# The entry of a feed-forward stage: four weight operands split ahead of the norm, three behind it, and the first products of two blocks put together

## The chip, the cores and the metric

The kernel runs on one core of a Trainium2 chip. The metric is the device time of one execution in microseconds (us); lower is better. The engines of the core work in parallel, each through its own queue in order: TensorE (PE, matmuls and transposes), VectorE (DVE), ScalarE (ACT), GpSimd (POOL) and SyncE (SP), which here only issues DMA transfers. Tiles live in SBUF (128 partitions), matmul results in PSUM (eight banks).

## The reference

One decoder layer on 512 tokens of width 1024, in float32: a time-mixing group and a sparse-attention group share one norm and one input projection, then comes the output projection and then a dense SwiGLU stage, in which the change lies:

```python
h = h + jnp.concatenate([y_r, y_n], axis=-1) @ w_out[l]
h = h + swiglu(rms_norm(h, norm_ffn[l]), w_gate[l], w_up[l], w_down[l])
return rms_norm(h, norm_final)

def rms_norm(x, g):
    y = xf * lax.rsqrt(jnp.mean(xf * xf, axis=-1, keepdims=True) + NORM_EPS)
    return (y * g.astype(jnp.float32)).astype(x.dtype)

def swiglu(x, w_gate, w_up, w_down):
    return (jax.nn.silu(x @ w_gate) * (x @ w_up)) @ w_down
```

The hidden width D_FF is 2816.

## The kernel before

**Split products.** Every float32 operand of a large product is split into a high half (rounded to a shorter float, by ScalarE, line 144) and a low half (the rest, by VectorE, line 146). `mm3` (lines 162 to 165) issues three matmuls for each pair: high by high, high by low, low by high. So each operand costs one ScalarE pass and one VectorE pass before TensorE can use it.

**The seven products.** The two matrices x @ w_gate and x @ w_up are formed together for 256 hidden columns at a time. The code calls such a piece a value of `q`; here it is called a block. There are eleven. For each, a Strassen-like scheme forms seven products in place of eight, of operands that are quarters or sums of quarters. On the activation side these are A11, A12, S1, S2, S3, S4 and A22, made once by `ffn_norm`. On the weight side they are B11, B21, T1, T2, T3, B22 and T4, made for each block by `weight_side`. The products of a block are taken in the order B11, B21, T2, T1, T3, B22, T4 (lines 1182 to 1203). `prod` issues 24 matmuls for each, into a PSUM bank of the tags pj, ra and s in turn. VectorE adds each result into the tiles u, g0, v and u1; ScalarE applies Silu.

**The norm.** `ffn_norm` is a generator; each step handles one tile of 128 tokens. ScalarE sums the squares (line 176) and takes the root (line 177), VectorE takes the reciprocal and then multiplies the rows by it and by the gain, which lies broadcast to all partitions in `gain2` (line 1072). TensorE transposes eight blocks of 128 (line 1082) into two ps_s banks, and ScalarE drains each bank in one pass of 512 columns into `raw` (line 1084). A11 and A12 are split from token tiles 0 and 1 directly. With tiles 2 and 3 the sums are formed by VectorE in place in `raw` (lines 1095 to 1100) and split one by one.

**The output projection ahead of it.** `accumulate` uses all eight PSUM banks: two for each token tile. For its last four blocks of rows it goes token tile by token tile and yields the tile's two banks. The caller adds them to `x2` (line 1159) and runs one step of the norm. `ahead` is called before that last part and traces `weight_side(0, 2)`: the loads of block 0, and its splits, of which the first two (B11, B21) get tiles of the tag b8 of their own. The other five use the tags whi and wlo, two buffers each, which the last weights of the output projection hold until its end.

**The loads of a block.** B11 and B21 are plain loads of w_gate into one tile of the tag wraw (three buffers), B22 a plain load of w_up into another. T1 and T3 are each a plain load from SyncE's queue and then, from GpSimd's queue, a load that adds in place (`accum_op`, lines 1137 and 1138). T2 = T1 + B22 and T4 = T2 + B21 are added by VectorE. For even blocks the tiles t1, t2, t3 have the tag t4 (four buffers), for odd blocks they are one large tile of the tag L (four buffers). The other L tiles at that time are `x2`, `raw`, `Aa` and the ring of the output projection, whose buffer `Ab` takes over.

**What orders the work.** Instructions are traced in program order. A planner that works with its own times for each instruction then puts them into the engines' queues, the earliest ready first and by priority; `tc.high_priority()` raises what is traced inside it. Before, the weight splits and the drains of the products have high priority, the norm does not. A tile of a tag waits until the last reader of the buffer's former tile is done.

## Time and profile before

| | |
|---|---|
| median of three runs | 770.64 us (769.45 to 771.62) |
| profiled execution | 770.73 us, span 769.0 us |
| TensorE busy | 738.6 us, 96% of the span, 6093 matmuls and transposes |
| VectorE, ScalarE, GpSimd busy | 543.3, 381.5 and 160.0 us |
| mean granted TensorE clock | 0.984 |
| moved by DMA | 82.83 MB, mean 108 GB/s |

The span runs from the first to the last instruction of the profiled execution; the time holds a little more around it. Starts of instructions are counted from the start of the span. A row of the timeline gives start, length, engine, line, operation, output and inputs with their shapes, how many such instructions it merges, and in brackets the engine's idle time before it and what ended that. A row of the waits gives who waited for whom, us in total, how often, and the longest. The chain of waits follows the work that ended last back from the end. In it, and in the groups, "L" is the name of a tile tag where it stands without a number, and a line of the code where a number follows. In the table of stretches the clock is that which the throttle granted to TensorE, 1.00 being full speed.

### The profile page before, as it was taken

Reading aid. Unit: us, or ns where it says so; the run is one execution under the profiler, and the core shown is the slowest. Engines: PE = TensorE matmul, PEld = TensorE weight load, DVE = VectorE, ACT = ScalarE, POOL = GpSimd, SP = SyncE. Lnnn points to the kernel's source line nnn. Section 1 sums busy time; section 2 is a strip of 40 time slices with the busy share of each in tenths; the row PEclk is TensorE's granted clock in tenths of the full one; section 3 lists DMA queues with packets and bytes.
Section 4 is the critical chain, followed back from the end, with each engine's and each line's share of the span. In section 5 each row is a group of like instructions: output and inputs, shape, how many; then the busy total and the mean of one; then the engine's idle time right before and its main releaser. Section 6 shows DMA issues by size and latency. Waiting matters only on the chain.

```text
span 769.0 us, 14989 instructions
## 1 busy us (share of the span) xinstructions
PE 738.6 (96%) x6093; PEld 648.1 (84%) x6093; DVE 543.3 (71%) x1052; ACT 381.5 (50%) x652; POOL 160.0 (21%) x258
## 2 busy tenths in 40 slices
PE   8999999998889999999996899999999999999996
PEld 7867888898877878867786899999999998888885
DVE  5488689789768987875659497888695994333235
ACT  7398643224277776676447344444443552233224
POOL 3210054058345542442001102020202000000000
PEclk9999999999989999999998999999999999999998
DMA  7722543100051000321218569696768444322102
GB/s 247 223 82 84 164 110 110 55 2 2 3 219 30 3 1 3 85 83 56 83 55 192 110 176 203 161 223 151 161 159 221 112 153 147 110 68 97 55 1 110
DMA packets 69243, 82.83 MB, mean 108 GB/s; under 512 B 4868, under 2 KB 62806, under 8 KB 69174
## 3 DMA queue, kind: packets, MB, share of 16 engines
q1 hardware_dynamic: 57558, 70.34, 28.5%
q0 software_dynamic: 11616, 11.54, 9.9%
q8 instruction: 48, 0.79, 0.4%
q14 instruction: 21, 0.17, 0.1%
HBM read 79.77 MB, written 2.10 MB: 106 GB/s over the span
## 4 chain that ended last, share of the span: by engine, by line
PE 74%; DVE 15%; DMA 6%; issue 2%; ACT 1%; POOL 0%; SPq 0%; DVEq 0%; POOLq 0%; ACTq 0%
PE ps_ra L165 7%; PE ps_ra L164 7%; PE ps_ra L163 6%; PE ps_pj L165 6%; PE ps_pj L163 6%; PE ps_pj L164 6%; PE ps_s L165 4%; PE ps_s L163 4%; PE ps_s L164 4%; PE ps_o L1001 3%; DVE wlo L146 3%; PE ps_pj L993 2%; DMA L<-in_w_up_dram 2%; DMA wraw<-in_w_up_dram 2%; DMA L<-in_w_gate_dram 2%
## 5 line engine op out<-in xcount | busy, mean ns | idle before, releaser
L144 ACT ACTIVATE whi<-wraw 128x1024 fp32r<-128x1024 f32 (+1 forms) x79 | 78.5, 1033 | 33.2 <-PE ps_s L165 8.2
L146 DVE TENSOR_TENSOR wlo<-wraw,whi 128x1024 fp32r<-128x1024 f32 (+1 forms) x62 | 77.7, 1284 | 14.9 <-ACT whi L144 11.3
L146 DVE TENSOR_TENSOR L<-b,L 128x512 fp32r<-128x512 f32 x24 | 16.2, 691 | 57.1 <-PE ps_rb L164 55.1
L990 POOL TENSOR_SCALAR whi<-whi,m,gates 128x128 f32<-128x128 f32 (+3 forms) x64 | 42.5, 679 | 36.9 <-DVE m L988 28.7
L144 ACT ACTIVATE L<-b 128x512 fp32r<-128x512 f32 x24 | 14.9, 632 | 70.0 <-PE ps_rb L164 65.1
L164 PE MATMUL ps_ra<-wlo,L 128*128 128x256 f32 (+1 forms) x140 | 47.6, 340 | 0.2 <-DVE wlo L146 0.2
L163 PE MATMUL ps_ra<-whi,L 128*128 128x256 f32 (+1 forms) x140 | 47.4, 340 | 0.2 <-ACT L L144 0.2
L165 PE MATMUL ps_ra<-whi,L 128*128 128x256 f32 (+1 forms) x140 | 47.0, 337 | 0.0
L165 PE MATMUL ps_pj<-whi,L 128*128 128x256 f32 (+1 forms) x140 | 46.3, 332 | 0.0
L164 PE MATMUL ps_pj<-wlo,L 128*128 128x256 f32 (+1 forms) x140 | 46.3, 331 | 0.0
L163 PE MATMUL ps_pj<-whi,L 128*128 128x256 f32 (+1 forms) x140 | 45.9, 332 | 0.0
L164 PE MATMUL ps_ra<-L,whi 128*128 128x256 f32 (+2 forms) x128 | 44.3, 346 | 1.0 <-DVE L L146 1.0
L163 PE MATMUL ps_ra<-L,whi 128*128 128x256 f32 (+2 forms) x128 | 44.1, 345 | 0.9 <-ACT L L144 0.9
L165 PE MATMUL ps_ra<-L,wlo 128*128 128x512 f32 (+2 forms) x120 | 41.2, 343 | 0.0
L987 ACT ACTIVATE whi<-whi,m 128x128 f32<-128x128 f32 (+3 forms) x64 | 35.4, 554 | 9.3 <-DVE m L986 8.1
L165 PE MATMUL ps_pj<-L,wlo 128*128 128x512 f32 (+1 forms) x112 | 38.8, 346 | 0.1
L163 PE MATMUL ps_pj<-L,whi 128*128 128x512 f32 (+1 forms) x104 | 36.3, 349 | 0.2 <-ACT whi L144 0.2
L164 PE MATMUL ps_pj<-L,whi 128*128 128x512 f32 (+1 forms) x104 | 35.9, 346 | 0.0
L986 DVE CUSTOM_DVE_ANT_0 whi<-ps_s,negb 128x128 f32<-128x128 f32 (+3 forms) x64 | 29.3, 484 | 5.9 <-PE ps_pj L993 2.5
L1137 POOL DMA_DIRECT2D t<-in_w_up_dram x6 | 7.9, 1322 | 115.1 <-DVE whi L146 50.4
L163 PEld LDWEIGHTS ps_ra<-whi,L 128*128 128x128 f32 x140 | 27.6, 197 | 3.1 <-ACT L L144 0.6
L164 PEld LDWEIGHTS ps_ra<-wlo,L 128*128 128x128 f32 x140 | 27.5, 196 | 3.0 <-DVE wlo L146 0.5
(627 smaller groups left out, 2462.4 us busy)
## 6 DMA issues: line engine op xcount, KB each, us to landing
wraw<-in_w_gate_dram SPq DMA_DIRECT2D x22, 512.0 KB
wraw<-in_w_down_dram SPq DMA_DIRECT2D x11, 1024.0 KB
wraw<-in_w_in_dram SPq DMA_DIRECT2D x9, 1024.0 KB
t<-in_w_up_dram POOLq DMA_DIRECT2D x12, 512.0 KB, 7.4
wraw<-in_w_up_dram SPq DMA_DIRECT2D x11, 512.0 KB
L<-in_w_up_dram POOLq DMA_DIRECT2D x10, 512.0 KB, 8.9
wraw<-in_w_out_dram SPq DMA_DIRECT2D x4, 1024.0 KB
wraw<-in_w_in_dram SPq DMA_DIRECT2D x6, 512.0 KB
```

Source lines behind the costliest of these rows:

```text
L144: ACT.activation(hi, src, AF.Copy)
L146: (POOL if pool else DVE).tensor_sub(lo, src, hi.bitcast(F32))
L163: PE.matmul(o, lh, rh, start=start, stop=False)
L164: PE.matmul(o, lh, rl, start=False, stop=False)
L165: PE.matmul(o, ll, rh, start=False, stop=stop)
L986: DVE.tensor_tensor_reduce(pr[:, i], pS[:, i], negb[:, S - n:S], scale=-1.0, scalar=3e38, op0=OP.add, op1=OP.min, accum_out=m[:, i, 0:1])
L987: ACT.activation(pr[:, i], pr[:, i], AF.Exp, scale=-1.0, bias=m[:, i, 0:1], accum_out=m[:, i, 1:2])
L990: POOL.tensor_scalar(pr[:, i], pr[:, i], m[:, i, 2:3], gv[:, 1 + b0 + i, h:h + 1], op0=OP.mult, op1=OP.mult)
L993: PE.transpose(pT[:, j], prr[:, x, j * 128:j * 128 + 128], ident)
L1001: PE.matmul(po[q, 2 * g:2 * g + 2], vtok[:, j % (t + 1), b0 + j // (t + 1), g], pTs[:, par, j], start=False, stop=g == 1 and bs[-1] == 1 a ...
L1137: POOL.dma_start(t1, quarter(w_up, 0), accum_op=OP.add)
```

## The change

- `t2` gets four buffers in place of three, and the scratch for DMA descriptors (`dynamic_dma_scratch_size`) is 2048 in place of 4096.
- The norm's weight `norm_ffn` is loaded as eight more of the small rows that are transposed at the start, so that it lies as one value for each partition; the broadcast tile `gain2` and its load go.
- In `ffn_norm` ScalarE multiplies the rows by the reciprocal root (a Copy with a scale), in place of VectorE. After the transposes ScalarE drains each block of 128 columns by a pass of its own, with the norm's weight as the scale: eight passes for each token tile in place of two.
- S1 gets a tile of its own and S3 is formed in place; the order of the splits is S2, S1, S3, S4, A22.
- `weight_side` becomes the class `Weights` with four parts: the constructor (loads of B11 and B21), `begin` (their splits), `load_rest` (the other loads), `middle` (T2 and T1), `end` (T3, B22, T4).
- For block 0, `ahead` splits B11, B21, T2 and T1, all into b8 tiles. `end` is traced after the norm, and its instructions on ScalarE and VectorE are queued behind the norm's last split.
- The additions to `x2` and the steps of the norm get high priority.
- The constructor and `begin` of block 1 are traced before that `end`, its other loads after block 0.
- The products go B11 and B21 of block 0, B11 and B21 of block 1, then the other five of block 0, the other five of block 1, and from block 2 on as before.

```diff
-    SB_BUFS = {"L": 4, "b8": 6, "t4": 4, "t2": 3, "wraw": 3, "whi": 2, "wlo": 2}
+    SB_BUFS = {"L": 4, "b8": 6, "t4": 4, "t2": 4, "wraw": 3, "whi": 2, "wlo": 2}
...
+                       ("norm_ffn", norm_ffn, 8)):
...
-    gain2 = st([128, D], "t4")
-    nc.sync.dma_start(gain2, bcast_row(norm_ffn))
...
+    last = []
     def ffn_norm(src):
...
-            DVE.scalar_tensor_tensor(xn, s, r, gain2, op0=OP.mult, op1=OP.mult)
+            ACT.activation(xn, s, AF.Copy, scale=r)
...
             def put(name, v):
-                split(v, A[name][0][:, :, c], A[name][1][:, :, c])
+                hi, lo = (o[:, :, c] for o in A[name])
+                last[:] = ACT.activation(hi, v, AF.Copy), DVE.tensor_sub(lo, v, hi.bitcast(F32))
...
-                ACT.activation(rv, p.rearrange("p (k n) -> p k n", n=128), AF.Copy)
+                for i in range(HK):
+                    ACT.activation(rv[:, i], p[:, i * 128:(i + 1) * 128], AF.Copy, scale=col("norm_ffn", kh * HK + i))
...
-                s3 = st([128, HK, 128], "t2")
-                DVE.tensor_sub(s3, a11, a21)
-                DVE.tensor_sub(a21, a22, a21)
-                DVE.scalar_tensor_tensor(a11, a21, -1.0, a11, op0=OP.mult, op1=OP.subtract)
+                s1 = st([128, HK, 128], "t2")
+                DVE.tensor_sub(s1, a22, a21)
+                DVE.tensor_sub(a21, a11, a21)
+                DVE.scalar_tensor_tensor(a11, s1, -1.0, a11, op0=OP.mult, op1=OP.subtract)
                 put("S2", a11)
-                put("S1", a21)
+                put("S1", s1)
+                put("S3", a21)
...
     def ahead():
-        first.append(weight_side(0, 2))
+        ws[0] = Weights(0)
+        ws[0].begin("b8")
+        ws[0].load_rest()
+        ws[0].middle("b8")
...
-        for f in range(2):
-            sl = slice(f * 512, f * 512 + 512)
-            DVE.tensor_add(x2[:, t, sl], banks[f], x2[:, t, sl])
-        next(norm)
+        with tc.high_priority():
+            for f in range(2):
+                sl = slice(f * 512, f * 512 + 512)
+                DVE.tensor_add(x2[:, t, sl], banks[f], x2[:, t, sl])
+            next(norm)
...
+    ws[1] = Weights(1)
+    ws[1].begin()
+    with tc.issue_after(last[0].ins), tc.issue_after(last[1].ins):
+        ws[0].end()
+    first_products(0)
+    first_products(1)
+    last_products(0)
+    for q in range(1, NF // 2):
+        if q > 1:
+            ws[q] = Weights(q)
+            ws[q].begin()
+        ws[q].load_rest()
+        ws[q].middle()
+        ws[q].end()
+        if q > 1:
+            first_products(q)
+        last_products(q)
```

`first_products(q)` holds the products with B11 and B21 and what follows them, `last_products(q)` the other five; their bodies are the lines 1181 to 1207 of before.

More of the change, by code (lines that the diff above doesn't have):

```diff
@@ L1150, in hybrid_layer, with __init__, quarter, put @@
-    first = []
+    class Weights:
+        def __init__(self, q):
+            def quarter(w, kh):
+                return w[kh * 512:kh * 512 + 512, q * 256:q * 256 + 256].rearrange("(k p) n -> p k n", p=128)
+            r = st([128, 2, HK, 256], "wraw")
+            self.b11, self.b21 = r[:, 0], r[:, 1]
+            nc.sync.dma_start(self.b11, quarter(w_gate, 0))
+            nc.sync.dma_start(self.b21, quarter(w_gate, 1))
+            self.q, self.quarter = q, quarter
+        def put(self, name, v, tag=None):
+            if tag is None:
+                tag = ("whi", "wlo")[turn2[0] % 2]
+                turn2[0] += 1
+            o = operand(tag)
+            split(v, *o)
+            setattr(self, name, o)
+        def begin(self, tag=None):
+            with tc.high_priority():
+                self.put("B11", self.b11, tag)
+                self.put("B21", self.b21, tag)
+        def load_rest(self):
+            self.b22 = st([128, 2048], "wraw")[:, 0:1024].rearrange("p (k n) -> p k n", n=256)
+            if self.q % 2:
+                tt = st([128, 4, HK, 256], "L")
+                self.t1, self.t2, self.t3 = (tt[:, i] for i in range(3))
+            else:
+                self.t1, self.t2, self.t3 = (st([128, HK, 256], "t4") for _ in range(3))
+            nc.sync.dma_start(self.t1, self.quarter(w_gate, 0))
+            nc.sync.dma_start(self.b22, self.quarter(w_up, 1))
+            nc.sync.dma_start(self.t3, self.quarter(w_up, 0))
+            with tc.high_priority():
+                POOL.dma_start(self.t1, self.quarter(w_up, 0), accum_op=OP.add)
+                POOL.dma_start(self.t3, self.quarter(w_up, 1), accum_op=OP.add)
+        def middle(self, tag=None):
+            with tc.high_priority():
+                DVE.tensor_add(self.t2, self.t1, self.b22)
+                self.put("T2", self.t2, tag)
+                self.put("T1", self.t1, tag)
+        def end(self):
+            with tc.high_priority():
+                self.put("T3", self.t3)
+                self.put("B22", self.b22)
+                DVE.tensor_add(self.t2, self.t2, self.b21)
+                self.put("T4", self.t2)
@@ L1198, in hybrid_layer @@
             DVE.tensor_add(u1, p, v)
-        p = prod(w["B22"], A["S4"])
+        p = prod(w.B22, A["S4"])
         with tc.high_priority():
@@ L1202, in hybrid_layer @@
         DVE.scalar_tensor_tensor(hq[:, :, 0:256], v, -1.0, g0, op0=OP.mult, op1=OP.mult)
-        p = prod(w["T4"], A["A22"])
+        p = prod(w.T4, A["A22"])
         with tc.high_priority():
```

72 lines of the change are left out of this document (21 added, 51 removed).

## The prediction

> **What bounds the kernel now.** The page comes first. Its row of TensorE (PE), busy tenths in 40 slices of 19.2 us:
>
> ```profile
> PE   8999999998889999999996899999999999999996
> ```
>
> Only a few stretches can give time back. The entry of the FFN, from 400 to 440 us, is too short to stand out in it. The table of stretches comes next (columns: stretch and its length, then busy us and instruction count of PE, PEld, DVE, ACT and POOL, then the granted clock, DMA share and GB/s):
>
> ```profile
> 405.00:410.00 5.00, 1.77 (x10) 1.21 (x10) 5.00 (x6) 5.00 (x10) 0.97 (x1) 0.98 0.60 158
> 410.00:415.00 5.00, 4.55 (x21) 4.55 (x22) 5.00 (x9) 2.14 (x6) 0.58 (x2) 0.50 1.02 269
> 420.00:425.00 5.00, 3.11 (x16) 2.71 (x17) 4.90 (x9) 4.28 (x7) 0.00 (x0) 0.85 0.33 53
> 435.00:440.00 5.00, 2.48 (x21) 2.27 (x20) 3.92 (x4) 1.06 (x1) 0.00 (x0) 1.00 0.74 119
> 460.00:480.00 20.00, 20.00 (x170) 20.00 (x169) 15.23 (x18) 8.84 (x10) 3.89 (x3) 1.00 0.91 212
> ```
>
> TensorE has holes and a halved clock here, while VectorE (DVE) is full. From 440 us on it is full: 170 matmuls in 20 us, 0.118 us each, so one product of 24 matmuls costs 2.82 us, and what is late at 438 stays late. TensorE's waits between 390 and 600 us, the four longest of six:
>
> ```profile
> PE ps_pj L165 <- DVE whi L146: 2.5, 1, 2.5
> PE ps_s L1082 <- ACT L L1084: 2.0, 1, 2.0
> PE ps_pj L164 <- DVE L L146: 1.8, 1, 1.8
> PE ps_ra L164 <- DVE L L146: 1.0, 1, 1.0
> ```
>
> They sum to 7.3 us. The clock adds to that: at 0.50 in one stretch of 5 us and 0.85 in another it wastes 2.5 and 0.75 us in these rows alone. So over 10 us look free. But the last and longest wait is not of the kind that the change fills. The chain of waits there (start, length, what):
>
> ```profile
> 424.51 0.70 DVE b L146
> 425.23 4.02 DMA L<-in_w_gate_dram
> ...
> 429.87 6.13 DMA L<-in_w_up_dram
> ...
> 437.22 1.23 DVE whi L146
> 438.49 0.39 PE ps_pj L165
> ```
>
> The reader is to see that the load of block 1's T1 starts 0.03 us after the last low half of the norm. T1 lies in an "L" slot; the four are held by x2, Aa, Ab and raw, and raw is free only when the norm has split its last operand. Call that moment N (425.2). From N it takes 13.3 us (load, accumulating load, add and split) until TensorE can start block 1's T2 at 438.49. TensorE has the same nine products to do before T2 of block 1 in both kernels: two of block 1 go ahead of five of block 0, none is added. So the change gains what it takes off N, less what it adds to the 13.3 us.
>
> **The change part by part.**
>
> *Start.* norm_ffn joins the small rows, ahead of the positions:
>
> ```profile
> 17.62 0.25 SPq L111 DMA_DIRECT2D t<-in_bv_dram  x1
> PE ps_s L676 <- DVE t L681: 1.0, 1, 1.0
> ```
>
> One more such issue on SyncE is 0.25 us. The slices from the second on are 9 in the row of TensorE, which hides it; uncovered it costs 0.25. The 512 KB broadcast of the gain goes; nobody waited for it: nothing. Its t4 slot lets block 2's T1 and T3 load early; nobody waits for those now either.
>
> *t2 with four buffers, smaller DMA scratch.* The first reorders work in the whole program; the longest wait of TensorE for a t2 tile before 390 us is the 1.0 above, so I take nothing, with 1 us to either side. The second would matter if it let one accumulating load at a time in flight; two are enough for what the rows below show. Nothing; at worst block 1's T3 comes late by some 3 us.
>
> *T1 and T2 of block 0 split early.* They leave the time after 402 and go to 376 to 390:
>
> ```profile
> 391.44 1.06 ACT L176 ACTIVATE t<-L 128x1024 bf16<-128x1024 f32 x1 [7.94 <-DVE L L1159]
> 392.61 1.28 ACT L177 ACT_TABLE_LOAD   x1
> 394.11 1.04 ACT L176 ACTIVATE t<-L 128x1024 bf16<-128x1024 f32 x1
> 395.27 0.29 ACT L177 ACTIVATE ss<-ss,eps 128x1 f32<-128x1 f32 x1
> 400.00 1.09 ACT L1084 ACTIVATE L<-ps_s 128x512 f32<-128x512 f32 x2 [0.18 <-PE ps_s L1082]
> 402.26 1.06 ACT L144 ACTIVATE wlo<-t 128x1024 fp32r<-128x1024 f32 x1
> 420.06 0.64 ACT L144 ACTIVATE L<-t 128x512 fp32r<-128x512 f32 x1
> 420.57 0.64 ACT L144 ACTIVATE kB<-L 128x512 fp32r<-128x512 f32 x1
> ```
>
> ScalarE (ACT) idles 7.94 us before 391.44, which hides the two high halves (1.06 less an overlap of 0.09 with the next, 1.9 us for both); without that cover they would cost 1.9. T3, B22 and T4 move behind N.
>
> *VectorE.* It is full from 400.44 to N:
>
> ```profile
> 400.44 1.28 DVE L1072 SCALAR_TENSOR_TENSOR b<-L,ss,t 128x1024 f32<-128x1024 f32 x1 [0.42 <-PE ps_s L1082]
> 407.44 1.22 DVE L146 TENSOR_TENSOR whi<-t,whi 128x1024 fp32r<-128x1024 f32 x1
> 408.58 1.22 DVE L1146 TENSOR_TENSOR t<-t,wraw 128x1024 f32<-128x1024 f32 x1
> ```
>
> Out go four low halves and T4's add (five, at 1.14 from start to start: 5.7) and two normalizing passes (at 1.2: 2.4), 8.1 us in all. In come the low halves of block 1's B11 and B21 (2.3) and one g0 add (0.6). VectorE alone would bring N to 425.2 - 8.1 + 2.9 = 420.0. The order S1, S3 has the same number of passes: nothing.
>
> *ScalarE takes over as the bound.* Shapes with and without a per-partition scale:
>
> ```profile
> L896 ACT ACTIVATE L<-ps_rb 128x128 f32<-128x128 f32 x4 | 1.1, 274 | 0.5 <-PE ps_rb L895 0.4
> L402 ACT ACTIVATE b<-ps_s,cs 128x512 f32<-128x512 f32 x8 | 5.1, 682 | 0.0
> L1084 ACT ACTIVATE L<-ps_s 128x512 f32<-128x512 f32 x8 | 4.3, 591 | 1.1 <-PE ps_s L1082 1.1
> ```
>
> A scale operand costs 0.09 us (682 less 591 ns); passes that follow each other overlap by 0.09 (the two drains at 400.00: 1.09 for two of 0.59). So a scaled 128x128 drain is 0.27 + 0.09 - 0.09 = 0.27 us, eight of them 2.2 per token tile where two drains took 1.09. Bounds: 0.20 (the 128x1 row of 0.29 less the overlap) gives 1.6, no overlap (0.36) gives 2.9. A normalizing pass on ScalarE is a 1.06 pass of 1024 with a scale, less the overlap: 1.06. Square, its read and Sqrt take 1.45 (394.11 to 395.27, plus 0.29). Per tile 4.7, for four 18.8. Then 14 high halves of 128x512 at 0.51 between starts, 7.1; the table load 1.3; B11 and B21 of block 1, 1.9; two copies of u, 1.0. Together 30.1 us from 391.44: 421.5. The last tile adds a chain that ScalarE waits in (three VectorE passes before S2, one more before S4), about 1.2 that other work only partly fills, and the last low half 0.7. N = 423.4, 1.8 earlier than now. Bounds by the two drain prices: 421.2 and 426.3. That ScalarE can begin at 391 rests on the high priority: now the first drains start at 400.00, 6 us after the first table load ends.
>
> The Trainium skill (ScalarE: Activation LUTs, What ACT_TABLE_LOAD costs) states 186 ns fixed, 0.833 ns an element and 93 ns more for each pointer operand, with 93 ns of overlap. By it a drain would be 0.29 us and N 0.7 later; the rows here give 0.09 for the operand too and a shorter fixed part, and I keep them.
>
> *From N to T2 of block 1.* The tied splits keep the two wraw slots of block 0 occupied. SyncE's queue now issues these early:
>
> ```profile
> 407.55 0.37 SPq L1124 DMA_DIRECT2D wraw<-in_w_up_dram  x1
> 409.83 0.37 SPq L1121 DMA_DIRECT2D wraw<-in_w_gate_dram  x1
> 410.24 0.50 SPq L1122 DMA_DIRECT2D wraw<-in_w_gate_dram  x1
> ```
>
> These three (B22 of block 1, B11 and B21 of block 2, 1.5 MB) can only go when B22 and T4 of block 0 are read: after two low halves, N + 2.4, and the add, N + 3.6. The accumulating load of T1 is issued at N + 4.6, so it now runs beside them. Now it takes 6.13 us with only its sibling beside it. Later in the loop, with plain loads in flight, it takes 9.67:
>
> ```profile
> 583.33 0.37 SPq L1124 DMA_DIRECT2D wraw<-in_w_up_dram  x1
> 583.96 9.67 DMA L<-in_w_up_dram
> L<-in_w_up_dram POOLq DMA_DIRECT2D x10, 512.0 KB, 8.9
> ```
>
> I take 8.9, the median of ten (the page's row), because plain loads surround most of them as they will here: 2.8 more, between 0 and 3.5. T2 of block 1 then starts at 423.4 + 13.3 + 2.8 = 439.5, 1.0 later than now.
>
> The Trainium skill (DMA: Bandwidth & Descriptors, Queues, rings and completion order) says that each DMA engine takes turns, packet by packet, between the queues with work. By it the accumulating load gets half of each engine while plain loads last, which would double the part of 6.13 that is transfer; 9.67 agrees with that direction.
>
> T3, B22 and T4 themselves (ScalarE 2.9, VectorE 4.5 with the add) lie under this wait. T3 is the tightest: done at about N + 2.3, needed two products after S2, about N + 3.6.
>
> *TensorE.* It now ends the accumulation of the output projection with these transposes:
>
> ```profile
> 403.65 1.03 PE L1082 MATMUL ps_s<-ident,b 128*128 128x128 f32 x8
> ```
>
> So it is free at about 404; A11 is there at about 405, four products last 11.3 and the transposes of tiles 2 and 3 some 2, so it is busy to about 419 instead of idle. S2 is complete at N - 2, five products take 14.1: 435.5. Then it waits 4.0 us for T2 of block 1. That is the sum: the holes move behind each other, and the end moves by +1.0. Against the profiled execution's 770.73 us (span 769.0, and 1.7 around it; the median of three is 770.64) that is 771.7.
>
> **The rivals.**
>
> *Faster: ScalarE packs well and the loads do not collide.* For it: VectorE alone would allow 420.0, and the DMA share was 0.74 at the end of the wait, not full. With N at 421.5 and 13.3 us, T2 starts at 434.8, 3.7 earlier: 767.0. With half the collision, 768.4. TensorE's own work allows no earlier than 404 + 1 + 2 + 25.4 = 432.4, so 764.6 is the floor: that would be the whole gap closed. It decides where N + collision falls under 422.9.
>
> *Slower: the wait grows and the clock falls.* If the drains do not overlap, or the norm and the products contend for the two ps_s banks, N stays at 425.2 and with 9.67 T2 starts at 442.0, 3.5 later: 774.3. TensorE then stands idle for well over 4 us. The stretch from 405 to 410, with 1.77 us of work in it, was followed by a clock of 0.50; some 3.2 us at half speed, an estimate midway between the 5 us of that stretch and the 1.5 us that a mean of 0.85 means in the other, cost 1.6 more: 775.9. Against it: the 2.5 us hole at 436 was followed by clock 1.00. It decides where N + collision exceeds 427.5.
>
> The Trainium skill (TensorE: Matmul & The Clock Gate, Part 1: The HAM clock gate) puts the fall after an idle window of about 3.4 us. By that my 4.0 us would cost the 1.6 too (773.3). This trace agrees for 405 to 410, but the clock of 0.85 from 420 to 425 stands beside holes of about 1 us, so the length alone does not decide.
>
> *No change because order wins:* if the scheduler puts block 1's splits or the tied ones otherwise than written, the same chain from raw still sets 438: within 1 us of now.
>
> **How the numbers follow.** About 0.3%, 2.3 us, is what a measurement tells from no change. T2 between 436.2 and 440.8: 0.41 in all, 0.35 of it the forecast and 0.06 the order rival; likeliest 771.7, own range 768.4 to 773.0. Faster rival 0.26; it needs both parts to go well. Slower rival 0.33, as contention, a held bank or the clock is enough alone. The range leaves out the floor and the extreme pile-up: 766.5 to 776.0.
>
> **What would show it.** Right: load of "L" from w_gate at 422 to 425, three wraw loads within 4 us behind it, the accumulating load above 8 us, TensorE waiting 2 us or more for block 1's T2, ScalarE full from 396 to N, the clock near 1.00 from 405 to 418. Wrong: N under 421; an accumulating load near 6 us; T2 of block 1 not waiting for raw; or a shift ahead of 390 us.

## The result and the profile after

The changed kernel takes 778.94 us (median of four runs, 777.37 to 781.05) against 770.27 us for the kernel before beside it: ratio 1.0113, 95% interval 1.0084 to 1.0141. It is slower by 1.1%. The forecast was 771.7 us with a range of 766.5 to 776.0, so the time lies above the range. The profiled execution is the slowest of the four: 781.05 us, span 779.3, 10.3 more than the span before.

First, where TensorE waits between 390 and 600 us (the waits of the changed kernel; who waited for whom, us in total, times, longest):

```profile
PE ps_s L1084 <- ACT L L1087: 3.8, 3, 2.8
PE ps_ra L166 <- DVE wlo L147: 3.1, 2, 1.8
PE ps_s L165 <- DVE kB L1079: 1.3, 1, 1.3
PE ps_s L164 <- ACT whi L145: 1.0, 1, 1.0
PE ps_s L164 <- ACT kB L1079: 1.0, 1, 1.0
PE ps_ra L166 <- DVE whi L147: 0.5, 1, 0.5
```

The longest is a transpose (L1084) that waits for ScalarE's scaled drains (L1087). Line 1079 is the split of the norm's operands. T2 of block 1, which the prediction put last, is not there: it starts at 449.79 without a wait.

The wait of the kernel before on which the prediction built was not for that product either. Its rows (timeline of the kernel before, VectorE and TensorE):

```profile
436.08 1.23 DVE L1141 TENSOR_TENSOR L<-L,wraw 128x1024 f32<-128x1024 f32 x1 [5.09 <-DMA L<-in_w_up_dram]
437.22 1.22 DVE L146 TENSOR_TENSOR whi<-t,whi 128x1024 fp32r<-128x1024 f32 x1
...
438.49 0.39 PE L165 MATMUL ps_pj<-L,whi 128*128 128x256 f32 x1 [2.52 <-DVE whi L146]
...
446.86 0.28 PE L163 MATMUL ps_pj<-gin,wlo 128*128 128x256 f32 x1
```

What TensorE waits for at 438.49 is the low half of T4 of block 0 (split from a `t` tile; block 1's sums lie in an `L` tile). VectorE, which works in order, has it behind the addition of block 1's T2 (L1141), and that waits for the accumulating load. T2 of block 1 itself (`wlo`, against S2 in `gin`) starts at 446.86, without a wait.

The table of stretches of the changed kernel shows what held its TensorE (stretch and length, busy us and count of PE, PEld, DVE, ACT, POOL, then clock, DMA share, GB/s):

```profile
405.00:410.00 5.00, 3.11 (x17) 2.22 (x15) 1.99 (x3) 5.00 (x12) 0.00 (x0) 1.00 0.00 0
410.00:415.00 5.00, 3.09 (x13) 2.49 (x14) 3.23 (x5) 5.00 (x18) 0.00 (x0) 0.65 0.01 2
415.00:420.00 5.00, 5.00 (x32) 5.00 (x31) 4.63 (x9) 4.97 (x12) 0.00 (x0) 0.66 0.01 3
420.00:425.00 5.00, 5.00 (x45) 5.00 (x44) 1.64 (x3) 2.33 (x8) 0.00 (x0) 1.00 0.00 0
425.00:430.00 5.00, 3.75 (x30) 3.34 (x28) 4.21 (x6) 4.97 (x10) 0.00 (x0) 1.00 0.11 21
430.00:435.00 5.00, 2.88 (x12) 2.48 (x13) 5.00 (x8) 4.22 (x6) 0.00 (x0) 0.70 0.64 206
435.00:440.00 5.00, 5.00 (x30) 5.00 (x29) 2.18 (x4) 0.63 (x1) 0.00 (x0) 0.62 0.50 168
480.00:520.00 40.00, 38.16 (x310) 37.96 (x309) 32.79 (x37) 15.42 (x17) 6.48 (x5) 0.96 0.77 185
```

ScalarE (ACT) is the full engine from 405 to 415, VectorE is not; then both are busy from 425 to 435 while TensorE has holes. The clock is 0.65 and 0.66 from 410 to 420, and 0.70 and 0.62 from 430 to 440. The last row was full before, with 338 matmuls; now it has 310. The chain of waits of the changed kernel (start, length, what) shows the end of the norm and what follows it:

```profile
436.58 0.70 DVE b L1079
...
437.36 3.65 DMA L<-in_w_gate_dram
...
441.68 1.29 POOL L L1148
442.97 4.72 issue
447.70 5.95 DMA L<-in_w_up_dram
...
453.75 1.07 ACT wlo L145
```

The accumulating load that starts at 447.70 is the second one, of T3; that of T1 starts at 441.68, and its first reader on VectorE at 447.41. The norm's last low half ends at 437.3, where the prediction had N at 423.4 and the kernel before 425.2. Part of that is a later start of the whole entry. VectorE's additions to x2 (the timeline, first of before, then of the changed kernel; the first pair and the last but one):

```profile
390.04 1.37 DVE L1159 TENSOR_TENSOR L<-ps_s,L 128x512 f32<-128x512 f32 x2 [5.09 <-PE ps_s L165]
...
401.64 0.68 DVE L1159 TENSOR_TENSOR L<-ps_o,L 128x512 f32<-128x512 f32 x1
```

```profile
393.58 1.29 DVE L1177 TENSOR_TENSOR L<-ps_s,L 128x512 f32<-128x512 f32 x2 [5.43 <-PE ps_s L166]
...
403.38 0.69 DVE L1177 TENSOR_TENSOR L<-ps_o,L 128x512 f32<-128x512 f32 x1 [0.40 <-PE ps_o L166]
```

From the last but one addition to the end of the span it is 367.4 us before (769.0 less 401.64) and 375.9 after (779.3 less 403.38). So of 10.3 us, 1.7 arise ahead of the entry and 8.5 from it on. The 1.7 are no fixed cost of the change: in `e3`, `e6`, `e7`, `e8` and `e16` below, which keep its four t2 buffers, its small scratch and its rows of `norm_ffn`, this addition stands at 401.5 to 402.3. The same distance is used below to compare profiles whose start is ordered differently.

The 8.5 do not all lie at the entry. VectorE's last addition of a product of the eleven blocks, with which the last stage (h @ w_down and the final norm) begins (timeline, first of before, then of the changed kernel):

```profile
642.49 0.69 DVE L1205 TENSOR_TENSOR t<-ps_ra,t 128x512 f32<-128x512 f32 x1 [0.85 <-PE ps_ra L165]
```

```profile
649.39 0.69 DVE L1231 TENSOR_TENSOR t<-ps_ra,t 128x512 f32<-128x512 f32 x1 [0.80 <-PE ps_ra L166]
```

From the last but one addition to x2 to this one it is 240.9 us before and 246.0 after, 5.2 more (240.85 and 246.01). From there to the end it is 126.5 and 129.9: 3.4 us of the slowdown arise in the last stage, which the change does not touch. `e2` shows where they come from.

### The profile page after: what moved, and what is told of

Read it like the earlier page. It is cut to its first block, busy times and chain, and to the rows that moved or that the text cites. A ratio compares the mean times of both kernels' runs of the same rounds, so it can differ in the third digit from the quotient of the medians.

```text
span 779.3 us, 14986 instructions
## 1 busy us (share of the span) xinstructions
PE 745.0 (96%) x6093; PEld 647.8 (83%) x6093; DVE 542.0 (70%) x1048; ACT 391.2 (50%) x681; POOL 158.4 (20%) x258
## 4 chain that ended last, share of the span: by engine, by line
PE 77%; DVE 12%; DMA 4%; ACT 3%; issue 2%; POOL 1%; SPq 0%; DVEq 0%; ACTq 0%; POOLq 0%
PE ps_pj L166 7%; PE ps_ra L166 7%; PE ps_ra L165 7%; PE ps_ra L164 7%; PE ps_pj L164 7%; PE ps_pj L165 7%; PE ps_s L164 4%; PE ps_s L166 4%; PE ps_s L165 4%; DVE wlo L147 3%; PE ps_o L1002 2%; PE ps_pj L994 2%; DMA L<-in_w_up_dram 2%; PE ps_s L981 1%; DMA wraw<-in_w_in_dram 1%
## 5 line engine op out<-in xcount | busy, mean ns | idle before, releaser
L147 DVE TENSOR_TENSOR wlo<-wraw,whi 128x1024 fp32r<-128x1024 f32 (+1 forms) x62 | 79.8, 1314 | 10.7 <-ACT whi L145 9.6
L166 PE MATMUL ps_pj<-whi,L 128*128 128x256 f32 (+1 forms) x140 | 48.1, 345 | 0.2 <-DVE L L147 0.2
L164 PE MATMUL ps_ra<-whi,L 128*128 128x256 f32 (+1 forms) x140 | 47.5, 339 | 0.3 <-ACT L L145 0.3
L164 PE MATMUL ps_pj<-whi,L 128*128 128x256 f32 (+1 forms) x140 | 47.4, 341 | 0.0
L165 PE MATMUL ps_ra<-L,whi 128*128 128x512 f32 (+2 forms) x120 | 41.3, 344 | 0.0
L166 PE MATMUL ps_pj<-L,wlo 128*128 128x256 f32 (+1 forms) x120 | 41.2, 343 | 0.0
L164 PE MATMUL ps_ra<-L,whi 128*128 128x512 f32 (+2 forms) x120 | 41.1, 343 | 0.0
L166 PE MATMUL ps_ra<-L,wlo 128*128 128x512 f32 (+2 forms) x112 | 39.2, 350 | 1.3 <-DVE wlo L147 1.3
L164 PE MATMUL ps_pj<-L,whi 128*128 128x512 f32 (+1 forms) x104 | 36.6, 352 | 2.2 <-ACT gin L448 2.2
L166 PEld LDWEIGHTS ps_pj<-whi,L 128*128 128x128 f32 x140 | 27.6, 197 | 3.6 <-DVE L L147 0.4
L164 PEld LDWEIGHTS ps_pj<-whi,L 128*128 128x128 f32 x140 | 27.8, 199 | 3.0
L165 PEld LDWEIGHTS ps_pj<-wlo,L 128*128 128x128 f32 x140 | 27.8, 198 | 2.9
```

Of the source, the lines that this page charges most:

```text
L147: (POOL if pool else DVE).tensor_sub(lo, src, hi.bitcast(F32))
L164: PE.matmul(o, lh, rh, start=start, stop=False)
L165: PE.matmul(o, lh, rl, start=False, stop=False)
L166: PE.matmul(o, ll, rh, start=False, stop=stop)
```

## The experiments

Ratios are to the kernel before, timed beside each experiment; where two experiments are compared, their intervals are.

### The two small resources

`e1`: the kernel before with the scratch of the change.

```diff
-dynamic_dma_scratch_size=4096
+dynamic_dma_scratch_size=2048
```

> The kernel before with one edit: the DMA scratch 2048 in place of 4096. Theory 'serial loads': two accumulating loads no longer fit in flight, so GpSimd issues the second of a pair 5 to 7 us after the first (it was 1.1 us) with a wait that no semaphore shows; T3 of the odd blocks comes some 5 us later, of which TensorE has little cover in the entry and at 580 to 600 us: 772 to 776 us. Rival 'no matter': the second load is needed two products later and stays hidden: within 1 us of 770.3. If GpSimd issues both within 2 us, the scratch has nothing to do with the 4.7 us waits of the changed kernel.

Measured 769.05 us, ratio 0.9995 (0.9985 to 1.0006): no change. But GpSimd's accumulating loads do change (timeline, first of the kernel before, then of this one):

```profile
429.87 1.29 POOL L1137 DMA_DIRECT2D L<-in_w_up_dram  x1 [13.80 <-DMA L<-in_w_gate_dram]
430.99 1.46 POOL L1138 DMA_DIRECT2D L<-in_w_up_dram  x1
```

```profile
428.43 1.29 POOL L1137 DMA_DIRECT2D L<-in_w_up_dram  x1 [7.24 <-DMA L<-in_w_gate_dram]
434.65 1.30 POOL L1138 DMA_DIRECT2D L<-in_w_up_dram  x1 [4.93 <-issue]
```

The second one starts 6.2 us after the first instead of 1.1: with the small scratch it is issued 0.3 us after the first has landed (428.43 and 5.91 by the chain of waits, 434.34). So the serial loads of the theory are there and their price is not. Here TensorE has the two products ahead of T3 as cover.

`e2`: the same with a fourth t2 buffer.

```diff
-"t2": 3
+"t2": 4
```

> The kernel before with scratch 2048 and four t2 buffers in place of three, to be read against e1. Theory 'front': the extra buffer reorders the work ahead of the FFN, and the first addition to x2 moves from 390.0 to about 393 us, as in the changed kernel (393.6): 2 to 3.5 us more than e1. Rival 'start noise': the 3.5 us of the changed kernel come from its first load landing 1.4 us late and from other new code, and e2 is within 1 us of e1.

Measured 772.86 us, ratio 1.0053 (1.0031 to 1.0074), 0.6% above `e1`. The front does come later, as the theory said: the first addition to x2 stands at 394.83 instead of 389.10 in `e1`. But that is one execution each, 1.9 us above its median here and 1.0 below it in `e1`. What comes back in every profile lies at the other end. From the last product of the blocks to the end of the span it takes 129.9 us (772.7 less 642.79) against 126.5 in `e1` (766.3 less 639.84). TensorE is full there in both, at full clock, and gets through fewer matmuls (stretches, first of `e1`, then of `e2`):

```profile
680.00:740.00 60.00, 60.00 (x266) 49.69 (x265) 20.87 (x23) 18.91 (x24) 0.00 (x0) 1.00 0.16 56
```

```profile
680.00:740.00 60.00, 60.00 (x259) 48.20 (x258) 18.86 (x21) 15.84 (x20) 0.00 (x0) 1.00 0.21 71
```

These are the same matmuls of 128x512, 0.227 us from start to start with three buffers and 0.233 with four; over the 528 of the last stage that is 3.5 us. All nine kernels with four t2 buffers have 258 or 259 matmuls in this stretch and 129.9 or 130.0 us behind the blocks, all eleven with three have 266 or 267 and 126.4 to 127.1, whatever their entry, scratch and parity. The 128x256 matmuls of the blocks go the other way, by less: from 520 to 600 there are 674 in `e1` and 678 in `e2`. So a buffer that nothing waits for makes another stage slower by 3.5 us. Why the same matmul takes longer is not shown; the tiles may lie elsewhere in SBUF, and no run varies that alone.

`e4`: the changed kernel with three t2 buffers (block 0's `g0` in t4) and the scratch at 4096.

> The changed kernel with three t2 buffers (block 0's g0 takes a t4 buffer) and the scratch at 4096, the entry as changed. Theory: the front is that of before (first addition to x2 at 390), the second accumulating load of a pair follows the first within 2 us: 3.5 to 6 us less than the changed kernel, 773 to 775.5, and what stays above 770.3 is the entry itself. Rival 'entry alone': the two resource edits cost nothing, and the time stays at 778 to 779.

Measured 775.90 us, ratio 1.0078 (1.0059 to 1.0097), 0.35% under the changed kernel with intervals that still touch. The additions to x2 are as late as in the changed kernel (last but one 403.3), so the front of before did not come back. Behind the entry the loads go in pairs again, and the stretch from 480 to 520 that had 310 matmuls has 338. But the 28 matmuls, 3.3 us at 0.118, are no gain of the whole: from the last but one addition to the last product of the blocks `e4` takes 247.3 us, the changed kernel 246.0. What `e4` gains is of the size of its shorter last stage (127.1 us against 129.9). Buffer and scratch were undone together here; that the scratch costs anything is not shown.

### The tie

`e3`: the changed kernel, with block 0's T3, B22 and T4 queued behind all five last operands of tile 3 instead of behind the one traced last.

```diff
-                last[:] = ACT.activation(hi, v, AF.Copy), DVE.tensor_sub(lo, v, hi.bitcast(F32))
+                last.append((ACT.activation(hi, v, AF.Copy), DVE.tensor_sub(lo, v, hi.bitcast(F32))))
...
-    with tc.issue_after(last[0].ins), tc.issue_after(last[1].ins):
+    with ExitStack() as tie:
+        for pair in last[-5:]:
+            for x in pair:
+                tie.enter_context(tc.issue_after(x.ins))
```

> The changed kernel with T3, B22 and T4 of block 0 queued behind all five last splits of the norm in place of that of A22 alone (A22 needs no sum, so its split stands first of the five in the queues). Theory 'tie too early': 3.0 us of ScalarE and 4.8 of VectorE leave the norm's tail, the norm ends 4 to 5 us earlier after the first addition to x2 (39 us in place of 43.7), and the time falls by 3 to 5 us: 774 to 776. Rival 'drains': the tail is set by tile 3's transposes, late at 423, and the eight drains behind them; then the norm ends at most 2 us earlier and the time falls by less than 1.5 us: 777.5 or more.

Measured 776.13 us, ratio 1.0092 (1.0077 to 1.0107). Why there is anything to gain shows in ScalarE's timeline of the changed kernel:

```profile
425.79 0.63 ACT L1079 ACTIVATE L<-L 128x512 fp32r<-128x512 f32 x1
426.32 1.05 ACT L145 ACTIVATE whi<-t 128x1024 fp32r<-128x1024 f32 x1
...
427.75 1.05 ACT L145 ACTIVATE wlo<-wraw 128x1024 fp32r<-128x1024 f32 x1
428.70 0.62 ACT L1079 ACTIVATE kB<-t 128x512 fp32r<-128x512 f32 x1
...
429.69 1.05 ACT L145 ACTIVATE whi<-t 128x1024 fp32r<-128x1024 f32 x1
...
435.92 0.63 ACT L1079 ACTIVATE b<-L 128x512 fp32r<-128x512 f32 x1 [1.67 <-DVE L L1104]
```

A22 is traced last but needs no sum, so the planner splits it first (425.79). The tied operands (line 145) follow at once and stand in front of S1, S3, S2 and S4 of the same tile. With the full tie, in `e3`, the norm ends at 431.67, 37.9 us after ScalarE's first pass of the norm (393.78) instead of 42.4 (394.90 to 437.3). And now the loads of the next operands go behind the norm, and the accumulating load of T1 runs beside them (chain of waits of `e3`):

```profile
436.15 8.76 DMA L<-in_w_up_dram
```

4.5 us less of norm give only 0.2% of time; the intervals overlap. TensorE's longest wait is now 3.9 us for the high half of T1 of block 1, which is split first from the accumulated tile, and 0.7 us more for its T2.

`e15` asks the same once ScalarE is free: the early tie, with VectorE's norm of `e9` below.

> The changed kernel with VectorE's norm and plain drains, and the tie as it was written (to the last operand traced alone). Theory (the tie lets T3, B22 and T4 in front of S1, S3, S2, S4 of tile 3 whatever makes the norm): the load into raw's slot starts 3 to 5 us later than with the full tie and VectorE's norm, and the time is 772.5 to 774.5 us. Rival (with ScalarE free, A22 is no longer split first, or there is room for the three operands): within 1 us of the full tie, 769.5 to 771.5 us.

Measured 774.07 us, ratio 1.0067 (1.0043 to 1.0090), against 1.0007 (0.9992 to 1.0022) with the full tie. The load into raw's slot starts at 429.5 instead of 426.1. Here the early tie costs 0.6%.

### ScalarE's part of the norm

`e7`, from `e3`, drains each bank in one unscaled pass; it leaves out the norm's weight, so it prices the eight passes and is no kernel to use:

```diff
-                for i in range(HK):
-                    ACT.activation(rv[:, i], p[:, i * 128:(i + 1) * 128], AF.Copy, scale=col("norm_ffn", kh * HK + i))
+                ACT.activation(rv, p.rearrange("p (k n) -> p k n", n=128), AF.Copy)
```

> The changed kernel with the tie to all five last operands, and each bank drained in one unscaled pass of 512 columns; the norm's weight is left out. Theory (the eight short drains of a tile, 2.2 us, lengthen ScalarE's part of the entry by about 1 us a tile): the norm ends 35 to 37 us after the first addition into x2 instead of 39.2, the first product starts 1 to 3 us sooner, and the time is 772 to 774.5 us. Rival (the drains run while ScalarE would wait, and the order of TensorE and the loads set the entry): the norm's end moves less than 1 us and the time stays at 775 to 777 us.

Measured 771.37 us, ratio 1.0016 (0.9997 to 1.0035): 0.76% off `e3`, the largest single piece of the slowdown. The load into raw's slot starts 25.3 us after the last but one addition (426.8 less 401.5) instead of 29.5 (431.8 less 402.3): 4.2 us, four tiles at 1.05. The first product starts at 409.23 instead of 412.41.

`e6`, from `e3`, keeps the scaled drains and gives the transposes of tiles 1 and 3 the two pj banks.

```diff
-                p = ps("s")
+                p = ps(("s", "pj", "s", "pj")[t])
```

> The changed kernel with the tie to all five last operands, and the transposes of tiles 1 and 3 in the two pj banks instead of the two s banks. Theory (the two s banks, each held by eight scaled drains, hold the transposes and with them the first products): TensorE's waits for ScalarE's drains at the transposes, 3.8 us in the changed kernel, fall under 1.5 us, the first product starts 2 to 3 us sooner after the first addition into x2 than with the tie alone, and the time is 1 to 3 us less: 773 to 775 us. Rival (ScalarE's whole work sets the norm's end, and TensorE only waits later for what it does sooner): the norm's end does not move, and the time is 775 to 777 us.

Measured 777.27 us, ratio 1.0103 (1.0070 to 1.0136): no gain. TensorE's waits from 395 to 480 us in `e6`:

```profile
PE ps_s L164 <- ACT L L1079: 5.8, 1, 5.8
PE ps_ra L164 <- ACT whi L145: 2.8, 1, 2.8
```

The waits of the transposes are gone, and the first product starts at 412.88 all the same, after 5.8 us for a high half of A11. The banks were not the limit, ScalarE's total was. My reading of the longest wait in the profile of after was wrong, and the rival right.

`e9`, from `e3`, undoes ScalarE's part: `gain2` is back, VectorE multiplies by the factor and the weight (before's line 1072), and each bank is drained in one pass. The early split, the full tie, the lead, four t2 buffers and the scratch of 2048 stay.

```diff
...
-            ACT.activation(xn, s, AF.Copy, scale=r)
+            DVE.scalar_tensor_tensor(xn, s, r, gain2, op0=OP.mult, op1=OP.mult)
...
```

> The changed kernel with the tie to all five last operands, and ScalarE's part of the norm undone: VectorE applies the factor and the norm's weight in one pass, as before the change, and each bank is drained in one pass of 512 columns. What stays of the change is the early split, the tie, the lead, four t2 buffers and the smaller scratch. Theory (ScalarE's normalizing pass and its eight drains a tile are the dear part): as with the plain drains alone (771.4 us) or better by the 1.06 us a tile of the normalizing pass: 768 to 771.5 us. Rival (VectorE becomes late: four passes of 1.2 us beside its splits): the norm ends later than with the plain drains, and the time is 772 to 775 us.

Measured 770.34 us, ratio 1.0007 (0.9992 to 1.0022). So with the tie mended and ScalarE's part undone, all of the slowdown is gone, though the fourth buffer and the small scratch are still there. It is gone as a sum: from the last but one addition to the last product of the blocks `e9` takes 6.9 us less than the kernel before (637.57 less 403.60, 234.0 against 240.9), and its last stage takes 3.4 more (129.9 against 126.5). Stretches of `e9`, and its first matmul of T2 of block 1:

```profile
410.00:415.00 5.00, 5.00 (x44) 5.00 (x44) 5.00 (x10) 2.64 (x6) 0.00 (x0) 1.00 0.03 6
...
435.00:440.00 5.00, 1.82 (x16) 1.62 (x14) 0.54 (x1) 0.46 (x1) 0.26 (x1) 1.00 0.76 138
440.00:445.00 5.00, 3.97 (x16) 3.53 (x17) 5.00 (x7) 2.60 (x3) 1.05 (x1) 0.56 0.69 101
```

```profile
441.83 0.58 PE L164 MATMUL ps_pj<-gin,wlo 128*128 128x256 f32 x1 [0.39 <-ACT wlo L145]
```

TensorE is full at full clock where it had holes, and the hole has moved to 435 to 441: 3.8 us of wait for T1 of block 1, whose accumulating load took 9.01 us, and 0.4 more for T2. That is the picture that the prediction drew for the change itself; but T2 of block 1 starts 5.0 us earlier than before (446.86), not 1.0 later.

### The priority and the lead

`e16`, from `e3`: the additions to x2 and the norm's steps without high priority. `e8`, from `e3`:

```diff
     first_products(0)
+    last_products(0)
     first_products(1)
-    last_products(0)
```

> The changed kernel with the full tie, and without the high priority of the additions to x2 and of the norm's steps. Theory (the priority lets ScalarE begin the norm early; it is part of what helps): ScalarE starts the norm later and the time is 777 to 780 us. Rival (the priority does nothing, since little else competes at the entry): within 1 us of the 776.1 us of the tie alone. Third (it is the priority that pushes the late work of the stage before behind the norm): 773 to 775 us.

> The changed kernel with the tie to all five last operands, and block 1's first two products put behind block 0's last five, so that only block 0's own two lead. Theory (the lead of block 1's products covers TensorE while the norm's last operands are made): TensorE meets S2 of tile 3 about 6.4 us sooner and waits there 3 to 6 us; the time is 779 to 782 us. Rival (the lead only moves the wait behind block 0's products, where T2(1) is late anyway): the time is 775 to 777 us, within 1 us of the tie alone.

`e16`: 776.43 us, ratio 1.0092 (1.0070 to 1.0114), the same as `e3`: the priority does nothing that can be measured. `e8`: 774.77 us, ratio 1.0069 (1.0047 to 1.0092), not slower than with the lead and perhaps a little faster. TensorE does wait sooner, 3.5 us for a high half of S1 (`PE ps_pj L164 <- ACT kB L1079`), but the 3.9 us for T1 of block 1 are gone; what it waits there, 1.3 us, is for the low half of T4 of block 0, which VectorE again has behind block 1's T2 addition. The lead moves a wait from one side of five products to the other.

### The slot of raw

`e5`: three t2 buffers, the scratch at 4096, the full tie, and the parity of the T tiles turned round, so that block 1's T1 and T3 lie in t4 and need no slot of raw:

```diff
...
-            if self.q % 2:
+            if self.q and self.q % 2 == 0:
...
```

`e10` is `e5` with VectorE's norm, `e11` is `e10` without the lead, `e12` is the kernel before with the parity alone.

> The changed kernel with three t2 buffers (block 0's g0 in t4), the descriptor scratch at 4096, the three late operands tied to all five last operands of tile 3, and the parity of the blocks' T tiles turned round: block 1 sums T1 and T3 in t4, blocks 2 and 4 in an L slot, so nothing of block 1 waits for raw's slot. Theory (the chain from the norm's end over the load into raw's slot to T2(1) costs TensorE time): T2(1) and T1(1) are split before the norm ends, the wait of ScalarE for the accumulated tile (4.02 us in the changed kernel, 2.96 us with the tie alone) is gone, and the time is 2 to 4 us under the 776.1 us of the tie alone: 772 to 774 us. Rival (TensorE has work of block 0 while that chain runs, so the chain is hidden): 775 to 776 us, within 1 us of the tie alone.

> As the changed kernel with the full tie and VectorE's norm, and with block 1's T1 and T3 summed in t4, so that they need no slot of raw, three t2 buffers (block 0's g0 in t4) and the scratch at 4096. Theory (two separate costs, ScalarE's passes and the chain behind the norm's end): 2 to 4 us under the same kernel with raw's slot, 765 to 769 us, so faster than the kernel before. Rival (once ScalarE is free, TensorE's work covers the chain, and the order of the work ahead of the entry costs 1 to 2 us as it did with the other slot alone): 769 to 772 us.

> The same with block 1's first two products behind block 0's last five. Theory (with the slot out of the way nothing of block 1 is late, and the lead only keeps four small tiles and two banks longer): within 1 us of the same kernel with the lead. Rival (the lead covers the wait for tile 3's operands): 2 to 4 us slower than with it.

> The kernel before with one edit: the parity of the T tiles turned round, block 1's in t4, blocks 2 and 4's in an L slot. Theory (in the kernel before too, the chain from the norm's end over raw's slot to T2(1) makes TensorE wait, 2.5 + 1.8 + 1.0 us): those waits go, and the time is 2 to 4 us less, 766 to 768 us against 769.5 to 770.5 us. Rival (the waits move to the next late thing, the operands of tile 3, or the front is reordered): 769 to 773 us.

| | us | ratio, interval |
|---|---|---|
| `e5` | 774.54 | 1.0059 (1.0038 to 1.0080) |
| `e10` | 766.67 | 0.9961 (0.9950 to 0.9973) |
| `e11` | 766.97 | 0.9967 (0.9952 to 0.9981) |
| `e12` | 770.64 | 1.0010 (0.9997 to 1.0023) |

`e5` is 0.33% under `e3`, between its theory and its rival, with intervals that just touch. `e10` is faster than the kernel before, and 0.46% under `e9`; the lead is again worth nothing (`e11`). But three things differ from `e3` and `e9`, the parity, the buffers and the scratch, and the buffers alone account for the gain: behind the blocks `e5` and `e10` take 126.5 and 126.4 us, `e3` and `e9` 130.0 and 129.9, and these 3.5 us are nearly the whole of the step from 770.34 to 766.67. So the parity is not shown to be worth anything. `e12`, the parity alone, shows no gain either, by its rival's mechanism. With the other parity the planner expects block 1's T1 early and queues the addition for T2 (L1141), at high priority, ahead of what is left of the norm. There VectorE waits 4.45 us (the profile names no releaser; the load of T1 is the likely one), and the norm (L1100) behind it (timeline of `e12`, then its stretches):

```profile
421.13 1.23 DVE L1141 TENSOR_TENSOR t<-t,wraw 128x1024 f32<-128x1024 f32 x1 [4.45 <-issue]
422.27 0.68 DVE L1100 SCALAR_TENSOR_TENSOR L<-L 128x512 f32<-128x512 f32 x1
```

```profile
420.00:425.00 5.00, 0.13 (x1) 0.13 (x1) 3.87 (x6) 1.94 (x4) 0.00 (x0) 0.94 0.59 97
425.00:430.00 5.00, 3.12 (x13) 2.83 (x14) 4.90 (x9) 3.53 (x5) 0.00 (x0) 0.50 0.00 0
```

TensorE has nothing to do for 5.8 us, since its next product needs an operand of tile 3, and then runs at a clock of 0.50.

### Single edits of the kernel before

`e13`: the eight rows of `norm_ffn` are loaded at the start and not used. `e14`: T2 and T1 of block 0 get b8 tiles too, and so can be split early:

```diff
-        first.append(weight_side(0, 2))
+        first.append(weight_side(0, 4))
```

`e17`: both. `e18`: `e14` with the other parity.

> The kernel before with the norm's weight loaded as eight more small rows at the start (unused; the broadcast stays). Theory (that load, ahead of everything, reorders the start and is why the additions to x2 come 1.8 us later in the changed kernel): the last but one addition to x2 moves from 401.6 to 403 us or later and the time is 771 to 772.5 us. Rival (the start hides it; the lateness is from the four t2 buffers and the other edits): 401 to 402 us and 769 to 770.8 us.

> The kernel before with one edit: T2 and T1 of block 0 get b8 tiles too and so can be split before the norm, as in the change; no tie, no lead, VectorE's norm. Theory (the early split alone is worth what it takes off VectorE in the entry, two low halves and an addition of 1.14 us each): the load into raw's slot starts 2 to 3.5 us sooner after the last but one addition to x2, and the time is 767 to 769 us. Rival (T3, B22 and T4 still stand ahead of the norm's last splits, and what is taken off one wait goes to the next): 769 to 771 us.

> The kernel before with both edits that were faster alone: the norm's weight as eight unused small rows (765.6 us), and T2 and T1 of block 0 in b8 tiles (765.0 us). Theory (two separate gains: an order of the start and the entry that happens to be better, and two splits less in the entry): the sum, 760 to 762.5 us. Rival (both are the same gain, another order of the same entry with a shorter stretch of halved clock): 764 to 766.5 us. Third (the orders do not add up at all): 767 to 770 us.

> The kernel before with T2 and T1 of block 0 in b8 tiles, and the parity of the T tiles turned round, so that block 1's T1 and T3 are summed in t4 and need no slot of raw. Theory (the slot's chain costs once the splits of block 0 are out of the entry's way, as with VectorE's norm and the full tie, where it was worth 3.6 us): 761 to 763.5 us. Rival (without a tie block 1's early splits stand in front of tile 3's operands, as in the kernel before with this edit alone, where TensorE waited 5.8 us for one of them): 765 to 768 us.

| | us | ratio, interval |
|---|---|---|
| `e13` | 765.64 | 0.9950 (0.9935 to 0.9965) |
| `e14` | 765.00 | 0.9940 (0.9922 to 0.9958) |
| `e17` | 764.44 | 0.9941 (0.9923 to 0.9959) |
| `e18` | 768.00 | 0.9974 (0.9959 to 0.9989) |

`e13` missed both expectations: the last but one addition did move to 403.0, as its theory said, but a load of 4 KB that nobody reads makes the kernel 0.5% faster. `e14`, at 765.00, is faster than its theory's 767 to 769, and not by its mechanism: the load into raw's slot starts 23.5 us after the last but one addition (425.9 less 402.4), as before (425.23 less 401.64). The two do not add (`e17`), as its rival said, and the other parity takes half of the gain back (`e18`). What `e13` and `e14` have in common is a shorter stretch of halved clock at the entry. TensorE's timeline, first of the kernel before, then of `e14`:

```profile
406.70 1.14 PE L1082 MATMUL ps_s<-ident,b 128*128 128x128 f32 x8 [2.01 <-ACT L L1084]
...
410.83 0.41 PE L165 MATMUL ps_pj<-L,b 128*128 128x256 f32 x1
411.04 0.41 PE L163 MATMUL ps_pj<-L,b 128*128 128x256 f32 x1
```

```profile
406.92 3.66 PE L1082 MATMUL ps_s<-ident,b 128*128 128x128 f32 x16 [2.35 <-ACT L L1084]
...
412.09 0.28 PE L165 MATMUL ps_pj<-L,b 128*128 128x256 f32 x1
412.21 0.28 PE L163 MATMUL ps_pj<-L,b 128*128 128x256 f32 x1
```

Before, products start 0.21 us apart until 416.6; in `e14` they are 0.12 apart from the beginning, and the slow time fell on transposes that cover a wait anyway. In `e13` the products are slow until 414.8. Busy time times the missing part of the clock, over the stretches of 5 us from 405 to 430, is 4.5 us before, 2.3 in `e13` and 1.0 in `e14`. That is argued from one profiled execution each, and the one of `e14`, at 769.47 us, is the slowest of its nine runs, so how the 5 us of the medians divide stays open.

## Why the prediction was wrong, step by step

- **"From N it takes 13.3 us ... until TensorE can start block 1's T2 at 438.49."** Misread, and the whole sum stands on it. At 438.49 TensorE goes on with T4 of block 0; block 1's T2 starts at 446.86, 8.4 us later. The forecast compared its own T2 of block 1, at 439.5 behind nine products, with a moment at which the kernel before had two of these nine and most of a third still to do. By its own picture the change should have gained some 7 us at this point, not lost 1.0; in `e9`, where the picture came about, T2 starts 5.0 us earlier than before.
- **"t2 with four buffers ... I take nothing, with 1 us to either side."** Failed. `e2`: +0.6% alone, and 3.5 us arise in the last stage, where a matmul of 128x512 takes 0.233 us instead of 0.227. The changed kernel pays 3.4 us there, a third of its 10.3. What failed is the argument from waits: that nobody waits for a t2 tile says what the buffer can gain, not what it costs elsewhere. The prediction looked for a shift ahead of 390 us only; that was 3.5 us at the first addition and 1.7 at the last but one, it does not come back in the kernels with the same front, and `e4` has it with three buffers.
- **"T3, B22 and T4 move behind N."** Failed. The tie is to the operand traced last, not to the one split last. 4.5 us of the norm's length (`e3`), worth 0.2% with intervals that overlap as long as ScalarE is full, 0.6% when it is not (`e15` against `e9`).
- **The price of a drain, 0.27 us, eight for 2.2.** Right: the eight of tile 3 took 2.17 (423.58 to 425.75).
- **ScalarE's sum of 30.1 us and N = 423.4.** The bound was the right engine, its size was short. In `e3`, the change as I had read it, the norm takes 37.9 us from ScalarE's first pass against 32.0 predicted (391.44 to 423.4). Two terms were missing: a second table load and block 0's and 1's Silu passes ahead of the end (1.28 and two of 0.52), and idle time of 4.7 us (37.0 less 32.28 busy from 394 to 431) where I had 1.2, the longest of it 2.25 us in which tile 3's transposes stand behind products on TensorE. With the late start of 3.5 and the tie's 4.5 this is the way from 423.4 to 437.3.
- **"A11 is there at about 405 ... TensorE is busy to about 419 instead of idle."** This is the step that cost most. A11 needs tiles 0 and 1, and its splits queue on ScalarE behind eight drains for each tile and B11 and B21 of block 1. The first product started at 413.54 and at half clock. I had costed the drains where the norm ends and not where it begins; `e7` puts 0.76% on them. ScalarE's total decided, not the two banks (`e6`), which I had named among the slower rival's reasons.
- **From N to T2 of block 1, an accumulating load of 8.9 us among plain loads, a wait of 4.0.** Not in the changed kernel: the early tie let the plain loads go at 428.3 to 432.2, before N, and the load of T1 took 5.7 (441.68 to 447.41). With the full tie it took 8.76 and 9.01, and TensorE waited 3.9 and 3.8 us for T1 of block 1, then 0.7 and 0.4 for T2 (`e3`, `e9`). By the Trainium skill (DMA: Bandwidth & Descriptors, Queues, rings and completion order) each DMA engine takes turns between the queues with work; the two lengths agree.
- **Scratch: "nothing; at worst block 1's T3 comes late by some 3 us."** Right for the kernel before (`e1`). In the changed kernel that tile does come late: ScalarE waits 4.02 us for it at 453.75. That this costs time is not shown: `e4`, with the larger scratch, gains no more than its shorter last stage.
- **The clock.** The slower rival had 1.6 us for one spell. In the changed kernel there are two, with 0.65 and 0.66 from 410 to 420 and 0.70 and 0.62 from 430 to 440, and neither follows a single hole of over 2.8 us.

The slower rival had the right sign and the halved clock, at 774.3 to 775.9 us; the two ps_s banks that it blamed are excluded by `e6`. That the time went beyond it is of the size of the last stage's 3.4 us, which stood at nothing. `e9`, with the tie mended and ScalarE's part undone, is at 770.34 us, near the forecast of 771.7, and that is luck: 6.9 us gained up to the last product of the blocks and 3.4 lost behind it, neither of which the prediction had.

## What to carry to other kernels

Work taken off a full engine has to be costed at the first consumer behind the new engine, not only at the end of the stage: here eight short passes instead of two, on an engine whose queue also makes the first operand, cost 0.76%. A tie to "the last" instruction must name the one that is issued last; the planner issues first what is ready first. A wait is named by its tile and its bank, not by its place in the story: the operands of the waiting row (`L` and `whi`, where T2 has `gin` and `wlo`) would have shown that 438.49 was another product. And the whole span has to be compared stage by stage, also behind the stage that was changed: there an extra buffer cost 3.5 us (`e2`), which in `e4`, `e5` and `e10` looks like a gain of whatever else was edited. An edit with no reason to matter moves the time by half a per cent either way (`e2`, `e13`), so a gain of that size needs an undo of each part before it is put down to a mechanism; of this change the early split alone, one number in the kernel before, gives 0.6% (`e14`), and the fastest kernel run, `e17`, is 764.44 us.

## What the runs showed of the hardware

With a descriptor scratch of 2048, GpSimd issues the second of two accumulating loads of 512 KB only 0.3 us after the first has landed (434.65 after 434.34 in `e1`, 439.74 after 439.43 in `e9`; "issue" waits of 4.72, 6.13 and 6.29 us in the changed kernel); with 4096 the two start 1.1 us apart. The same matmuls of 128x512, at a clock of 1.00 and with no wait, start 0.227 us apart with three t2 buffers and 0.233 with four (266 against 259 in 60 us); why stays open. Transposes slow down with the clock like matmuls: 16 in 3.66 us in a stretch with a clock of 0.67 (`e14`) against 8 in 1.03 at 1.00 (the changed kernel, 403.88). A hole of some 2 us at the same place (2.01 and 2.35) halves the clock of the products in the kernel before and only of transposes in `e14`. The Trainium skill (TensorE: Matmul & The Clock Gate, Part 1: The HAM clock gate) says that the window of some 3.4 us over which the clock is decided runs freely, so that what is slow depends on where in it the work lands; these traces agree, and no run here varies that alone.
